# Projection to v and dt as seven block products instead of eight, moved behind the first B, C and x tiles, in a hybrid SSD and attention layer

## The chip, the cores and the metric

The kernel runs on one core of one Trainium2 chip. The metric is the device time of one execution in microseconds (us), the median of several runs. The engines named below are TensorE (PE in the profile; its weight loads are PEld), VectorE (DVE), ScalarE (ACT), GpSimd (POOL) and SyncE (SP, which issues most DMAs). An engine works through its own instructions in order; engines wait for each other through semaphores.

## The reference

One layer of a bidirectional encoder over 512 tokens and a model width of 1024, in float32. All projections of the input come from one matrix product; its columns are split into the parts that the two branches use:

```python
u = h @ w_in                      # x: 512 x 1024
z, xbc, dt_f_raw, dt_b_raw, q, k, v, gate_logits = split(u, ...)
y_ssd = ssd_branch(z, xbc, dt_f_raw, dt_b_raw, ...) @ w_proj_ssd
y_att = attention_branch(q, k, v) @ w_proj_attn
```

In the SSD branch `xbc` (the columns x, B and C) passes a centred convolution over five tokens and SiLU; `dt` is a softplus of its raw columns, 32 heads for each of two directions. From dt come the decays: cumulative sums of `dt * a` over chunks of 128 tokens. The attention branch needs q, k and v (12 heads of 64, so v has 768 columns). Gate, output projection, two LayerNorms and a feed-forward layer of width 4096 follow.

What the change touches is the product of x (512 x 1024) with the 832 columns of v (768) and dt (64).

## The kernel before

**Precision.** A float32 operand is split into a high part `h` (a copy rounded to the matmul's float32r) and a low part `l` = operand minus `h`. A product is three matmuls: h·h, l·h and h·l. The high part is a cast on ACT, the low part a subtraction on DVE (in `Stream.prep`, L107 and L108, for weights; in `split_x`, L227 and L228, for x).

**Weights.** The class `Stream` brings weight tiles in the order of their use: `load` issues the DMA into one of three buffers `wraw`, `prep` splits it into one of two buffers each of `wh` and `wl`, `get` hands out one tile, splits the next and loads up to three ahead. The split is traced under a raised priority: `PRIO = 100` places ahead of where it stands in the program.

**The v/dt stage** (`v_dt_stage`) comes first. Its weights are eight tiles of 128x832, one for each 128 rows (k) of x. For each k and each of four token chunks, x is the stationary operand and the weights move, in three matmuls of 512 columns (`ps_va`, v) and three of 320 (`ps_vb`, the rest of v and dt). All eight PSUM banks accumulate over k. At the end ACT copies the banks to `vs`, four DMAs write v to `dr_v` in DRAM, where the attention picks it up much later, and a chain on ACT and DVE makes dt and `tok` from the dt columns (L266 to L280), with two loads of activation tables (L275, L276).

**B, C and x0 to x3** follow (`plan0`). Each is a column tile: the weights are stationary, x moves, 24 matmuls of 512 columns (`quarters`, L138). `evict` reads the PSUM bank: the convolution is one ACT pass, four DVE steps (L317), a Tanh on ACT (L318) and one more DVE step (L319). Three PSUM banks with the tag `mm` take these tiles in turn. Behind x1 the first matmuls of `cumsum_stage` (L286 to L294) read `tok`; the transposes (L299) follow within x2.

**Order.** Instructions of an engine are ordered by a planner that takes by priority, which is the order of tracing unless raised, what its own timing has ready. From the SSD groups on, TensorE's order is the written one (`manual_schedule`); for the stages above it is the planner's, with `issue_after` as a tie for the cumulative sums. Behind that come four SSD groups with further column tiles between their steps, the attention with projections, and the feed-forward layer. The last one (from 680 us) already multiplies in blocks: seven products per block pair, with sums of blocks by DVE and by adding DMAs on POOL (L1208), and operands split on ACT and DVE (L1233 to L1240).

Of the kernel before, what the change touches and what calls it, by code (L numbers as in the profile page):

```python
# [16 lines left out]
P = 128  # L17
# [17 lines left out]
TAIL = 4  # L35
QT = 1.36
# [9 lines left out]
def hybrid_layer_kernel(ctx: ExitStack, tc: tile.TileContext, t: dict, out: bass.AP):  # L46
# [27 lines left out]
    class Stream:  # L74
# [6 lines left out]
        def load(self, i):  # L81
            if i < len(self.srcs) and i not in self.raw and (self.end is None or i < self.end):
                ap, width, hold = self.srcs[i]
                r = wp.tile([P, 1024], F32, name=f"wraw{i}", tag="wraw", bufs=3)
                if i:
                    dma.dma_start(r[:, :width], ap)
                else:
                    act.dma_start(r[:, :512], ap[:, :512])
                    dma.dma_start(r[:, 512:width], ap[:, 512:])
                self.raw[i] = r  # L90

        def prep(self, i):
            if i < len(self.srcs) and i not in self.hl and (self.end is None or i < self.end):
# [11 lines left out]
                with tc.high_priority(PRIO):  # L105
                    if i:
                        act.copy(h[:, :width], r[:, :width])  # L107
                        dve.tensor_sub(l[:, :width], r[:, :width], f32(h[:, :width]))  # L108
                    else:
                        dve.tensor_copy(h[:, :512], r[:, :512])  # L110
                        self.second = act.copy(h[:, 512:width], r[:, 512:width])
                        dve.tensor_sub(l[:, :512], r[:, :512], f32(h[:, :512]))
                        dve.tensor_sub(l[:, 512:width], r[:, 512:width], f32(h[:, 512:width]))
                self.hl[i] = (h, l)

# [39 lines left out]
    yp_ctx = ExitStack()  # L155
    yp = yp_ctx.enter_context(tc.tile_pool(name="yp", bufs=1, side="right"))
    ys = [yp.tile([P, S], F32, name=f"y{j}", tag="y", bufs=17) for j in range(16)]
# [15 lines left out]
    sp = pa.enter_context(tc.tile_pool(name="sp", bufs=2))  # L173
# [21 lines left out]
    for k in range(KT):  # L195
        ws.add(t["w_vd"][k], 832)
# [11 lines left out]
    xr = []  # L208
    for k in range(KT):
        xr.append(sp.tile([P, S], F32, name=f"xr{k}", tag="x", bufs=8))  # L210
        if k:
            dma.dma_start(xr[k], t["xT"][:, k, :])
        else:
            dma.dma_start(xr[k][:, :256], t["xT"][:, k, :256])
            dma.dma_start(xr[k][:, 256:], t["xT"][:, k, 256:])
        if k < 3:
            ws.load(k)
    dma.dma_start(vec, t["vec"])
    dma.dma_start(dtv, t["dtv"].to_broadcast([P, P]))
    dma.dma_start(tri, t["tri"][:, 1:6, :])  # L220
    dma.dma_start(ident, t["tri"][:, 0, :])

    def split_x(k):
        if k < KT:
            with tc.high_priority(PRIO):
                for cs in ((slice(0, S),) if k else (slice(0, 256), slice(256, S))):
                    act.copy(xh[k][:, cs], xr[k][:, cs])  # L227
                dve.tensor_sub(xl[k], xr[k], f32(xh[k]))  # L228
# [10 lines left out]
    def v_dt_stage():  # L239

        pv = [ps_tile("mm", f"ps_va{i}", 3) for i in range(3)] + [ps_tile("tp", "ps_va3", 3)]
        pd = [ps_tile("tp", f"ps_vb{i}", 3) for i in range(2)] + [ps_tile("y", f"ps_vb{i}", 2) for i in (2, 3)]
        split_x(0)
        ws.prep(0)
        with tc.issue_after(ws.second.ins):
            split_x(1)
        for k in range(KT):
            wh, wl = ws.get()
            split_x(k + 2)
            for i in range(NCH):  # L250
                xk = [(xh[k][:, i * P:(i + 1) * P], xl[k][:, i * P:(i + 1) * P])]
                if k:
                    mm3(pv[i], xk, [(wh[:, :512], wl[:, :512])], False, k == KT - 1)
                    mm3(pd[i][:, :320], xk, [(wh[:, 512:832], wl[:, 512:832])], False, k == KT - 1)
            if k == 0:
                for n, (l, r) in enumerate(((xh, wh), (xl, wh), (xh, wl))):
                    for ps_, cs in ((pv, slice(0, 512)), (pd, slice(512, 832))):
                        for i in range(NCH):
                            pe.matmul(ps_[i][:, :cs.stop - cs.start], l[0][:, i * P:(i + 1) * P], r[:, cs], start=(n == 0), stop=False)
        na = sp.tile([P, 64], F32, name="na", tag="acc", bufs=2)  # L260
        act.activation(na, dtv[:, 64:128], AF.Exp)
        dve.tensor_scalar(na, na, -1.0, None, op0=ALU.mult)
        tl = lambda n: sp.tile([P, NCH, 64], F32, name="dt" + n, tag=n, bufs={"G1": 4, "U": 2, "sq": 2}.get(n, 1))
# [1219 lines left out]
```

## Time and profile before

| | |
|---|---|
| median of three runs | 989.39 us (988.30 to 989.45) |
| the profiled execution | 988.57 us, span 986.8 us |
| TensorE busy | 976.1 us, 99% |
| VectorE busy | 787.0 us, 80% |
| ScalarE busy | 597.2 us, 61% |
| GpSimd busy | 71.7 us, 7% |
| granted TensorE clock | 0.997 |

The span runs from the first to the last instruction; the time around it (1.8 us) belongs to the execution but to no instruction. Busy time of TensorE counts overlapping matmuls once, so 99% means hardly any gap, and not that each matmul is at its peak. The page also has 40 slices with tenths of busy time, groups of instructions, the chain of work that ended last and the DMA queues. A row of a timeline gives start and duration in us, then engine, line, operation, output<-inputs, shape and count, and in brackets the idle time before it and who ended it. A row of one tile's instructions gives shortest, median and longest duration in ns, and the first and the last start in us.

### The profile page before, as it was taken

The numbers are of one execution on the slowest core, as the hardware profiler recorded it, in microseconds if no ns is written. First come the engines' busy times: TensorE is split into PE (matmuls) and PEld (weight loads), VectorE is DVE, ScalarE is ACT, GpSimd is POOL, SyncE is SP. The second block draws the span as 40 slices with busy tenths as digits, with TensorE's granted clock in tenths as the row PEclk, the third lists the DMA queues.
The fourth block names the chain that finished last, engine by engine and source line by source line (L and its number), as shares of the span: only waits on it lengthen the run. The fifth ranks groups of instructions, "written<-read, shape, count | busy, mean of one in ns | idle before, by whom it ended". The sixth has DMA issues, their size and how long they took to land.

```text
span 986.8 us, 14803 instructions
## 1 busy us (share of the span) xinstructions
PE 976.1 (99%) x5471; PEld 835.6 (85%) x5471; DVE 787.0 (80%) x1224; ACT 597.2 (61%) x1140; POOL 71.7 (7%) x74
## 2 busy tenths in 40 slices
PE   9999999999999999999999999999999999999997
PEld 7888888888888888788778888889989998989986
DVE  4296998698998899997788258498898898898757
ACT  4454696369856995695765344147666566666620
POOL 0000100030012101202000000000200110110000
PEclk9999999999999999999999999999999999999998
DMA  7436367325752484374773249313953854671322
GB/s 246 155 116 174 111 201 215 108 86 171 213 154 86 151 241 139 129 245 139 257 221 108 83 156 308 130 44 111 251 151 129 211 131 168 175 170 44 110 83 86
DMA packets 56808, 153.09 MB, mean 155 GB/s; under 512 B 7456, under 2 KB 8736, under 8 KB 56480
## 3 DMA queue, kind: packets, MB, share of 16 engines
q1 hardware_dynamic: 53136, 139.30, 43.6%
q0 software_dynamic: 3456, 12.58, 6.9%
q8 instruction: 43, 0.70, 0.3%
q10 hardware_dynamic: 144, 0.26, 0.1%
q14 instruction: 29, 0.24, 0.1%
HBM read 128.25 MB, written 11.30 MB: 141 GB/s over the span
## 4 chain that ended last, share of the span: by engine, by line
PE 91%; DVE 4%; issue 2%; ACT 1%; DMA 1%; POOL 0%; SPq 0%; DVEq 0%; POOLq 0%; ACTq 0%
PE ps_pa L138 9%; PE ps_x L138 8%; PE ps_z L138 8%; PE ps_x L1124 8%; PE ps_g L138 8%; PE ps_z L1124 4%; PE ps_k L138 3%; PE ps_q L138 3%; PE ps_pX L148 2%; PE ps_pX L149 2%; PE ps_pX L150 2%; PE ps_y L1124 2%; PE ps_B L138 2%; PE ps_yo L550 2%; PE ps_u L138 2%
## 5 line engine op out<-in xcount | busy, mean ns | idle before, releaser
L108 DVE TENSOR_TENSOR wl<-wraw,wh 128x1024 fp32r<-128x1024 f32 (+1 forms) x113 | 140.5, 1249 | 75.6 <-ACT wh L107 58.6
L107 ACT CAST wh<-wraw 128x1024 fp32r<-128x1024 f32 (+1 forms) x113 | 116.5, 1036 | 92.7 <-PE ps_vb L150 16.6
L1240 DVE TENSOR_TENSOR cl<-wq_B,ch 128x1024 fp32r<-128x1024 f32 x42 | 51.2, 1220 | 14.1 <-ACT ch L1239 13.6
L1239 ACT CAST ch<-wq_B 128x1024 fp32r<-128x1024 f32 x42 | 44.1, 1050 | 23.4 <-PE ps_pX L150 16.8
L138 PE MATMUL ps_pa<-yh,wh 128*128 128x512 f32 x128 | 51.7, 404 | 0.0
L138 PE MATMUL ps_g<-xh,wh 128*128 128x512 f32 x128 | 50.6, 395 | 0.0
L138 PE MATMUL ps_x<-xh,wh 128*128 128x512 f32 x128 | 50.5, 394 | 0.0
L138 PE MATMUL ps_z<-xh,wh 128*128 128x512 f32 x128 | 50.4, 393 | 0.0
L138 PE MATMUL ps_g<-xl,wh 128*128 128x512 f32 x128 | 49.9, 390 | 0.0
L138 PE MATMUL ps_x<-xl,wh 128*128 128x512 f32 x128 | 49.9, 390 | 0.0
L138 PE MATMUL ps_z<-xl,wh 128*128 128x512 f32 x128 | 49.9, 389 | 0.0
L1208 POOL DMA_DIRECT2D wq_B<-wq_B x24 | 20.8, 866 | 393.1 <-DMA wq_B<-in_w_dn_dram 227.0
L138 PE MATMUL ps_pa<-yl,wh 128*128 128x512 f32 x128 | 48.4, 393 | 0.0
L317 DVE SCALAR_TENSOR_TENSOR acc<-ps_x,vec,acc 128x510 f32<-128x510 f32 (+1 forms) x64 | 47.6, 743 | 0.8 <-ACT acc L315 0.3
L519 ACT ACTIVATE U<-bc,acr 128x128 f32<-128x128 f32 x128 | 42.3, 391 | 8.7 <-DMA bc<-dr_acr 8.6
L521 DVE SCALAR_TENSOR_TENSOR U<-bc,acr,U 128x128 f32<-128x128 f32 x128 | 43.1, 376 | 0.0
L525 ACT ACTIVATE G<-cb,tok 128x128 f32<-128x128 f32 x128 | 41.7, 390 | 0.0
L148 PE MATMUL ps_pX<-ch,ah 128*128 128x512 f32 x96 | 37.6, 392 | 0.0
L149 PE MATMUL ps_pX<-cl,ah 128*128 128x512 f32 x96 | 37.6, 392 | 0.0
L150 PE MATMUL ps_pX<-ch,al 128*128 128x512 f32 x96 | 37.3, 389 | 0.0
L1233 ACT CAST ah<-r 128x1024 fp32r<-128x1024 f32 x21 | 22.1, 1054 | 21.4 <-PE ps_pX L149 14.3
L138 PE MATMUL ps_pa<-yh,wl 128*128 128x512 f32 x128 | 34.8, 392 | 0.0
(857 smaller groups left out, 2787.5 us busy)
## 6 DMA issues: line engine op xcount, KB each, us to landing
wraw<-in_w_in_dram SPq DMA_DIRECT2D x68, 512.0 KB, 3.7
bc<-dr_acr SPq DMA_DIRECT2D x64, 256.0 KB, 4.2
pr<-in_w_up_dram SPq DMA_DIRECT2D x28, 512.0 KB, 5.5
wq_B<-in_w_dn_dram SPq DMA_DIRECT2D x24, 512.0 KB, 4.4
wq_B<-wq_B POOLq DMA_DIRECT2D x24, 512.0 KB, 4.7
be<-dr_ear SPq DMA_DIRECT2D x32, 256.0 KB, 5.2
wraw<-in_w_ps_dram SPq DMA_DIRECT2D x16, 512.0 KB, 3.9
dr_gate<-g SPq DMA_DIRECT2D x16, 256.0 KB, 2.2
```

The source lines that it names most:

```text
L107: act.copy(h[:, :width], r[:, :width])
L108: dve.tensor_sub(l[:, :width], r[:, :width], f32(h[:, :width]))
L138: ins = pe.matmul(ps, l, r, start=(first and n == 0), stop=(last and n == len(seq) - 1))
L148: pe.matmul(ps, lh, rh, start=(first and i == 0), stop=False, skip_group_check=not check)
L149: pe.matmul(ps, lh, rl, start=False, stop=False, skip_group_check=not check)
L150: ins = pe.matmul(ps, ll, rh, start=False, stop=(last and i == n - 1), skip_group_check=not check)
L317: dve.scalar_tensor_tensor(acc[:, o0:o1], ps[:, i0:i1], w(k), acc[:, o0:o1], op0=ALU.mult, op1=ALU.add)
L519: act.activation(U[:, ch(c)], bb[:, ch(c)], AF.Identity, bias=acr[:, c, 32 + h:33 + h])
L521: dve.scalar_tensor_tensor(U[:, ch(c)], bf[:, ch(c)], acr[:, c, h:h + 1], U[:, ch(c)], op0=ALU.subtract, op1=ALU.min)
L1124: pe.matmul(ps[:, LO], w_[:, wk], src[:, x, k0 + k, cs], start=(first and i == 0), stop=(i == 11), skip_group_check=not first)
L1239: act.copy(h, w[:, j, :])
L1240: dve.tensor_sub(l, w[:, j, :], f32(h))
```

## The change

The product of x and the 832 columns is cut in halves: tokens (2 x 256), features (2 x 512) and columns (2 x 416, `VC`). Instead of eight block products there are seven, with sums and differences of blocks as operands (the scheme of Strassen in Winograd's form). Three of them (1, 2 and 4) use a plain block of x, whose split exists; the other four split a sum.

- **B and C come first.** `first_tiles` computes both at once, in six matmuls per k, so that the slices of x are used as they come. The first halves (k = 0 to 3) of their two weight tiles are loaded ahead of x1, the second halves behind x3 (`load_rest`, `prep_rest`). x0 follows; then the seven products, then x1 to x3.
- **Raw x stays** in one tile `xr`, and four quarters of it (`a11` to `a22`) are overwritten with sums by DVE (`v_prepare`). The four weight blocks `wvq` are loaded whole, 128 x 1664 each; DVE adds b12 and then b22 to b11, POOL's adding DMAs add b22 to b12 and later b21 to b11.
- **A product** is two chunks of 128 tokens, each twelve matmuls of 416 columns. Two chains of PSUM banks, X and Z, go on accumulating over several products; after each product ACT copies the running sum out (`vo`, with sign) and a DMA stores it to its block of `dr_v` or adds it there (products 3, 7 and 2, on POOL). The last 64 columns of the right half are dt: DVE adds them up in `xb`.
- **Preparation** of the product after next is traced behind each product, in buffers of two each for the weight parts (`vh`, `vl`) and the x parts (`vs`), with raised priority. The evictions of B, C and x0, with their convolutions, are traced before the first product.
- **TensorE's order** is the written one through all of this. Behind x1 come the cumulative sums, as before.
- **Buffers.** The stage's pool `vq` is closed after the seven products; the buffers of y and most of those of the SSD groups (`sp.late`) are placed where it was, with waits tile by tile. Those of x, B, C, acc and sq are in a pool of their own (`se`) from the start.

```diff
-    for k in range(KT):
-        ws.add(t["w_vd"][k], 832)
...
+        if k == 0:
+            ws.load(0)
+            ws.load(1)
+        elif k == 3:
+            ws.load_rest(0)
+            ws.load_rest(1)
     dma.dma_start(vec, t["vec"])
     dma.dma_start(dtv, t["dtv"].to_broadcast([P, P]))
...
+    for i, c in ((0, 0), (0, 1), (1, 1), (1, 0)):
+        wvq[i, c] = vq.tile([P, 4, VC], F32, name=f"wv{i}{c}")
+        dma.dma_start(wvq[i, c].rearrange("p k n -> p (k n)"), t["w_vd"][i, c])
+        if i == c == 0:
+            ws.load(2)
+            dma.dma_start(tri, t["tri"][:, 1:6, :])
+            dma.dma_start(ident, t["tri"][:, 0, :])
...
+    def first_tiles():
+        split_x(0)
+        ws.prep(0)
+        split_x(1)
+        ws.prep(1)
+        for k in range(2, KT):
+            split_x(k)
+            if k == 3:
+                ws.prep_rest(0)
+                ws.prep_rest(1)
+        two = [(kind, ps_tile("mm", f"ps_{kind}0", 3), ws.get(0)) for kind in "BC"]
         for k in range(KT):
+            wk = slice(k * P, (k + 1) * P)
+            for n, (wx, xx) in enumerate(((0, xh), (0, xl), (1, xh))):
+                for kind, ps, w in two:
+                    pe.matmul(ps, w[wx][:, wk], xx[k], start=(k == 0 and n == 0), stop=(k == KT - 1 and n == 2))
+        return two
...
+        straight = {1: (0, 0), 2: (4, 0), 4: (4, 2)}
+        w_of = {1: b11, 5: b11, 6: b11, 3: b22, 7: b12, 2: b21, 4: b11}
+        a_of = {5: a21, 6: a21, 3: a21, 7: a11}
+        outs = {1: ("X", 0, 0, 1.0), 5: ("Z", 1, 1, 1.0), 6: ("X", 0, 1, -1.0), 3: ("Z", 0, 1, 1.0), 7: ("X", 1, 1, -1.0), 2: ("Z", 0, 0, 1.0), 4: ("X", 1, 0, 1.0)}
+        order = [1, 5, 6, 3, 7, 2, 4]
...
+        def v_prepare(p):
+            with tc.high_priority(PRIO):
+                h = vq.tile([P, 4, VC], F32R, name=f"vh{p}", tag="vh", bufs=2)
+                l = vq.tile([P, 4, VC], F32R, name=f"vl{p}", tag="vl", bufs=2)
+                sa = None
+                if p in a_of:
+                    sa = vq.tile([P, 2, 4, 256], F32R, name=f"vs{p}", tag="vs", bufs=2)
+                    act.copy(sa[:, 0], a_of[p])
+                    dve.tensor_sub(sa[:, 1], a_of[p], f32(sa[:, 0]))
+                act.copy(h, w_of[p])
+                dve.tensor_sub(l, w_of[p], f32(h))
+                if p == 1:
+                    dve.tensor_sub(a21, a21, a22)
+                    dve.tensor_add(b11, b11, b12)
+                elif p == 5:
+                    dve.tensor_sub(a21, a21, a11)
+                    dve.tensor_add(b11, b11, b22)
+                    pool.dma_start(b12, b22, accum_op=ALU.add)
+                elif p == 6:
+                    dve.scalar_tensor_tensor(a11, a21, -1.0, a22, op0=ALU.mult, op1=ALU.subtract)
+                    dve.tensor_add(a21, a12, a21)
+                    pool.dma_start(b11, b21, accum_op=ALU.add)
...
+                    for n, (x_, w_) in enumerate(((ah, h), (al, h), (ah, l))):
+                        pe.matmul(ps, x_, w_[:, k, :], start=(first and k == n == 0), stop=(k == 3 and n == 2), skip_group_check=not first)
+                i = row * 2 + q
+                st = vq.tile([P, VC], F32, name=f"vo{p}{q}", tag="vo", bufs=4)
+                act.activation(st, ps, AF.Copy, scale=sign)
+                dst = dr_v[i * P:(i + 1) * P, col * VC:min(768, (col + 1) * VC)]
+                src = st[:, :dst.shape[1]]
+                if p in (3, 7, 2):
+                    pool.dma_start(dst, src, accum_op=ALU.add)
+                else:
+                    dma.dma_start(dst, src)
+                if col:
+                    if p in (5, 6):
+                        dve.tensor_add(xb[:, i, :], st[:, VC - 64:], dtv[:, 0:64])
+                    else:
+                        dve.tensor_add(xb[:, i, :], st[:, VC - 64:], xb[:, i, :])
+
+        v_prepare(1)
+        x0 = tile_task("x", 0)
+        next(x0)
+        v_prepare(5)
+        for kind, ps, w in two:
+            evict(kind, 0, ps)
+        for _ in x0:
+            pass
+        for n, p in enumerate(order):
+            v_product(p)
+            if n + 2 < 7:
+                v_prepare(order[n + 2])
...
+    with tc.manual_schedule(engines={mybir.EngineType.PE}):
+        v_dt_stage(first_tiles())
+        vq_ctx.close()
...
+        sp.late = pa.enter_context(tc.tile_pool(name="sp", bufs=2, reuse_waits="tile"))
+        cums = cumsum_stage()
+        for n, _ in enumerate(bg(plan0[3:])):
+            if n in (3, 6):
                 next(cums, None)
```

More of the change, by code (lines that the diff above doesn't have):

```diff
@@ L35 @@
 TAIL = 4
+VC = 416
 QT = 1.36
@@ L105, in prep @@
                 with tc.high_priority(PRIO):
-                    if i:
+                    if i > 1:
                         act.copy(h[:, :width], r[:, :width])
@@ L154, in hybrid_layer_kernel @@
     edge.tile([P, 56], F32, name="edge")
-    yp_ctx = ExitStack()
-    yp = yp_ctx.enter_context(tc.tile_pool(name="yp", bufs=1, side="right"))
-    ys = [yp.tile([P, S], F32, name=f"y{j}", tag="y", bufs=17) for j in range(16)]
+    vq_ctx = ExitStack()
+    vq = vq_ctx.enter_context(tc.tile_pool(name="vq", bufs=1, side="right"))
     ps_ctx = ExitStack()
@@ L172, in hybrid_layer_kernel, with tile @@
     xp = pa.enter_context(tc.tile_pool(name="xp", bufs=1))
-    sp = pa.enter_context(tc.tile_pool(name="sp", bufs=2))
+    se = pa.enter_context(tc.tile_pool(name="se", bufs=2))
+    class Work:
+        late = None
+        def tile(self, shape, dt, name, tag, bufs):
+            home = se if tag in ("sq", "x", "acc", "B", "C") else self.late
+            return home.tile(shape, dt, name=name, tag=tag, bufs=bufs)
+    sp = Work()
     plan0 = [("B", 0), ("C", 0)] + [("x", j) for j in range(4)]
@@ L261, in v_dt_stage @@
         act.activation(na, dtv[:, 64:128], AF.Exp)
         dve.tensor_scalar(na, na, -1.0, None, op0=ALU.mult)
-        tl = lambda n: sp.tile([P, NCH, 64], F32, name="dt" + n, tag=n, bufs={"G1": 4, "U": 2, "sq": 2}.get(n, 1))
-        xb, e, w1, d1 = tl("G1"), tl("G2"), tl("U"), tl("sq")
-        for i in range(NCH):
-            dve.tensor_add(xb[:, i, :], pd[i][:, 256:320], dtv[:, 0:64])
-            vs = sp.tile([P, 2, S], F32, name=f"vs{i}", tag="be", bufs=2).rearrange("p a s -> p (a s)")
-            act.copy(vs[:, 512:768], pd[i][:, 0:256])
-            act.copy(vs[:, 0:512], pv[i])
-            dma.dma_start(dr_v[i * P:(i + 1) * P, :], vs[:, :768])
+        e, w1, d1 = [vq.tile([P, NCH, 64], F32, name="dt" + n) for n in ("e", "w1", "d1")]
@@ L583, in run @@
                     lb = False
-    v_dt_stage()
-    for n, _ in enumerate(bg(plan0)):
-        if n == 4 * CS + 3:
-            cums = cumsum_stage()
-        if n in (4 * CS + 3, 4 * CS + 6):
-            with tc.issue_after(last_mm[0].ins):
+    with tc.manual_schedule(engines={mybir.EngineType.PE}):
+        v_dt_stage(first_tiles())
+        vq_ctx.close()
+        yp_ctx = ExitStack()
+        yp = yp_ctx.enter_context(tc.tile_pool(name="yp", bufs=1, side="right", reuse_waits="tile"))
+        ys = [yp.tile([P, S], F32, name=f"y{j}", tag="y", bufs=17) for j in range(16)]
+        sp.late = pa.enter_context(tc.tile_pool(name="sp", bufs=2, reuse_waits="tile"))
+        cums = cumsum_stage()
+        for n, _ in enumerate(bg(plan0[3:])):
+            if n in (3, 6):
                 next(cums, None)
```

84 lines of the change are left out of this document (47 added, 37 removed).

## The prediction

> **What bounds the kernel now.** I read the head of the page first, then the windows of the first 70 us, because the change lies there. All times are microseconds.
>
> ```profile
> span 986.8 us, 14803 instructions
> PE 976.1 (99%) x5471; PEld 835.6 (85%) x5471; DVE 787.0 (80%) x1224; ACT 597.2 (61%) x1140; POOL 71.7 (7%) x74
> ```
>
> ```profile
> core 0: us, PE busy (x) PEld busy (x) DVE busy (x) ACT busy (x) POOL busy (x), PEclk, DMA share, GB/s
> 0.00:10.00 10.00, 8.80 (x34) 5.60 (x34) 4.02 (x7) 4.58 (x7) 0.34 (x6) 1.00 0.76 252
> 10.00:20.00 10.00, 9.85 (x53) 8.70 (x53) 6.01 (x11) 5.50 (x9) 0.00 (x0) 1.00 0.81 289
> 20.00:30.00 10.00, 10.00 (x55) 8.80 (x54) 2.88 (x3) 1.90 (x3) 0.00 (x0) 1.00 0.36 120
> 30.00:40.00 10.00, 10.00 (x55) 8.82 (x54) 2.71 (x5) 2.68 (x4) 0.00 (x0) 1.00 0.33 105
> 40.00:50.00 10.00, 10.00 (x48) 8.38 (x47) 2.85 (x7) 7.63 (x14) 0.00 (x0) 1.00 0.61 224
> 50.00:60.00 10.00, 10.00 (x46) 8.29 (x45) 9.72 (x14) 4.94 (x8) 0.00 (x0) 1.00 0.43 145
> 60.00:70.00 10.00, 10.00 (x52) 8.40 (x51) 9.82 (x15) 5.54 (x9) 0.00 (x0) 1.00 0.33 107
> ```
>
> The reader should see three things. TensorE is the bound everywhere, so a saved matmul is saved time unless TensorE then waits. The only stretch with idle VectorE (DVE) is the v/dt stage, at 2.7 to 2.9 of 10. From 50 on, where the convolutions of B, C and x run, DVE is at 9.7 to 9.8 of 10. And DMA is busiest (0.76, 0.81) in the first 20 us, when x and the first weights come in.
>
> The matmul spacing comes from first and last starts, and from the chain of waits, which merges matmuls that follow each other.
>
> ```profile
> 4.71 1.46 PE L259 MATMUL ps_va<-wh,xh 128*128 128x512 f32 x4
> ...
> 9.60 0.40 PE L148 MATMUL ps_va<-wh,xh 128*128 128x512 f32 x1
> ...
> 57.92 0.39 PE L138 MATMUL ps_x<-xh,wh 128*128 128x512 f32 x1
> ...
> 63.36 0.38 PE L286 MATMUL ps_cum<-tok,tri 128*128 128x128 f32 x2
> ```
>
> ```profile
> L148 PE MATMUL ps_va<-wh,xh x28: 393/393/398, 9.6 to 40.4; 128*128 128x512 f32 x28
> ```
>
> ```profile
> 47.20 5.44 PE ps_C L138 x24
> 52.64 10.88 PE ps_x L138 x48
> ```
>
> L148 recurs 28 times from 9.6 to 40.4, once per chunk of three 512-column and three 320-column matmuls: 30.8 / 27 = 1.14; one wait of about 0.3 at 10 us is in it, without it 1.13. The 32 chunks therefore cost 36.1. A column tile (24 matmuls of 512) costs 5.44. B starts at 41.6, the tile x1 at 57.92, and the cumulative sums, which need dt, at 63.36. These last two times are what the change must move.
>
> **The change, part by part.**
>
> **TensorE.** 192 matmuls become 168 of 416 columns. No row shows 416, but it lies exactly halfway between 512 and 320, so by interpolation 24 of them cost as much as four chunks, 4.51, and seven products 31.6. Removed: 4.5. Bounds: 24 x 0.227 = 5.44 a product if 416 paid as 512 (then 38.1, a loss of 2.0), and 24 x 0.15 = 3.6 if it paid as 320 (a gain of 11). I take the middle because both forms scale with columns.
>
> **The start.** Now v needs a new slice of x every 4.5; the B and C tiles in front need one every six matmuls, 1.36. So x must arrive faster.
>
> ```profile
> 7.14 0.62 ACT L227 CAST xh<-xr 128x512 fp32r<-128x512 f32 x1 [1.73 <-DMA xr<-in_xT_dram]
> ...
> 8.15 0.89 ACT L107 CAST wh<-wraw 128x832 fp32r<-128x832 f32 x1 [0.39 <-DMA wraw<-in_w_vd_dram]
> ```
>
> ```profile
> L227 ACT CAST xh<-xr x9: 405/616/622, 4.0 to 13.2; 128x512 fp32r<-128x512 f32 x7, 128x256 fp32r<-128x256 f32 x2
> L228 DVE TENSOR_TENSOR xl<-xr,xh x8: 681/684/693, 5.2 to 14.5; 128x512 fp32r<-128x512 f32 x8
> ```
>
> Slice x1 was cast at 7.14 with 0.95 MB queued up to and with it, the next weight at 8.15 with 1.38 MB, the last slice at 13.2 with 3.38 MB. So from 7.14 on 0.4 MB land per us. In the new order 1.05 MB stand up to x1 (7.4), 3.15 to the last slice (12.6), 4.16 to the first v weight block (15.2), 4.68 to x0's weights (16.5), 5.93 and 6.78 to the blocks (0,1) and (1,1) (19.6 and 21.7). B's first matmul needs the whole slice 0, so about 5.0. At k = 1 it waits for the cast of x1 (8.0); from there seven steps of 1.36 and 0.2 for x1's low half give an end of B and C at 17.8, against 15.9 without waits: 1.9 lost. Before, step k = 0 took 4.89 (9.60 - 4.71) instead of 4.51, and the wait at 10 us was 0.3; 0.7 of that old loss goes. x0's weight cast (16.5 + 1.05) is just in time, and x0 ends at 23.25. If x1's cast goes ahead of C's weight cast on ScalarE (ACT), C's first matmul waits until 8.6 and B and C end at 19.2. If the transfers do not limit, they end at 15.9.
>
> [...]
>
> **Side engines.** Each product needs a high and a low part of a weight block (128x1664), four sums of x quarters and two of weight blocks are made on DVE (two more by adding DMAs), and four products split an x operand of 1024.
>
> ```profile
> L107 ACT CAST wh<-wraw x12: 887/890/1050, 8.2 to 56.7; 128x832 fp32r<-128x832 f32 x7, 128x1024 fp32r<-128x1024 f32 x5
> L108 DVE TENSOR_TENSOR wl<-wraw,wh x11: 1024/1026/1226, 9.1 to 55.3; 128x832 fp32r<-128x832 f32 x7, 128x1024 fp32r<-128x1024 f32 x4
> ```
>
> ```profile
> 52.28 3.10 DVE L317 SCALAR_TENSOR_TENSOR acc<-ps_B,vec,acc 128x510 f32<-128x510 f32 x4
> ...
> 56.42 0.69 DVE L319 SCALAR_TENSOR_TENSOR B<-B,acc 128x512 f32<-128x512 f32 x1
> ```
>
> DVE: 0.684 at 512 and 1.226 at 1024 give 1.06 ns a column, so 1.90 at 1664. ACT: 0.616 and 1.05, so 1.59. DVE work in the stage: nine times 1.90 (seven low parts, two block sums) and eight times 1.22 (four low parts of x, four x sums) is 26.9, one of the 1.22 before 16.8 (the first block's landing and its high part, 15.2 + 1.59). Beside it stand three convolutions at 3.7 (11.1), low weights of x0, x1 and x2 (3.7) and eight additions to the dt columns at 0.22 (1.8): 43.5. TensorE, unhindered, gives from 14.5 (x split: ten low parts of 0.69 that DVE makes one after the other behind x1's cast) to 60.3 (cumulative sums: 23.25 + 31.6 + 5.44) 45.8. So DVE, idle before, is nearly full; it is the new second bound. Followed product by product with the preparations ahead of the convolutions, DVE is never free between 16.8 and 37: the third product's low weights are there at 32.7, wanted at 32.6; the fourth's low x at 37.0, wanted at 37.0. One convolution step that slips in costs 0.75. I take 0.8, one step, for such waits; bounds 0 and 7.9 (the slower rival below: 62.8 - 54.85).
>
> The kernel holds a stage of the same make, seven products with split operands and adding DMAs, further on. Its six 40-us windows from 680 to 920 sum to:
>
> ```profile
> sum 240.00, PE 240.00 PEld 220.57 DVE 209.14 ACT 156.13 POOL 20.80; mean PE 40.00 PEld 36.76 DVE 34.86 ACT 26.02 POOL 3.47
> ```
>
> DVE at 87% there leaves TensorE without idle time. That speaks for a small wait, but 43.5 of 45.8 is 95%.
>
> **Adding DMAs.**
>
> ```profile
> wq_B<-wq_B POOLq DMA_DIRECT2D x24, 512.0 KB, 4.7
> ...
> dr_v<-vs SPq DMA_DIRECT2D x4, 384.0 KB, 4.0
> ```
>
> ```profile
> L714 SPq DMA_DIRECT2D vc<-dr_v x1: 560/560/560, 487.9 to 487.9; - x1
> ```
>
> An add of 512 KB lands after 4.7, so one of 832 KB within some 7.6; b12 is wanted three products (13) later, b11 likewise: hidden. The eight stores and six adds into the v scratch have until 488. POOL has no work in any window from 10 to 70. On SP a store waits for its eviction, and a weight load queued behind it comes up to a product (4.5) late; the next weights are wanted two tiles (10.9) on. All this costs nothing; with the cover gone a late add costs at most its 7.6. The waits for the stage's released buffers fall on tiles first written behind the cumulative sums, more than a tile after the last reader: nothing.
>
> **dt.** The last dt addend comes from the fifth product, two products (9.0) and one tile (5.4) before the cumulative sums.
>
> ```profile
> 41.77 0.23 DVE L266 TENSOR_TENSOR dtG<-ps_vb,dtv 128x64 f32<-128x64 f32 x1 [0.90 <-PE ps_vb L150]
> ...
> 45.95 1.28 ACT L275 ACT_TABLE_LOAD   x1
> ...
> 50.80 0.43 DVE L280 TENSOR_TENSOR tok<-tok,na 128x256 f32<-128x256 f32 x1
> ```
>
> That chain took 9.5 (41.77 to 51.23) and was done 12 before its use. Now 14.4 are there. In the forecast it is ready: 0.
>
> **Sum.** x1 starts at 23.25 + 31.6 + 0.8 = 55.65 instead of 57.92: 2.3 less. Profiled time 988.57 - 2.3 = 986.3. That execution lies 0.8 below the median of 989.39, and the median less 2.3 is 987.1; I take 986.6.
>
> **Rivals.**
>
> **Whole eighth** (15%). Transfers do not limit and DVE never waits: 41.6 - 4.5 is kept, and up to 0.7 of the old start loss: 988.57 - 4.5 = 984.1, with the same 0.3 towards the median 984.4. For it: from 7.14 on the rows land 0.4 MB per us. Against it: the 1.36 pace of B and C in front. [...]
>
> **dt late** (24%). The convolutions of B, C and x0 stand before the dt chain in the program. If DVE does them first it is full to 16.8 + 42.3 = 59.1, and the chain from its first table load on (45.95 to 51.23: 5.3) ends at 64.4; TensorE, in written order, stands at the cumulative sums from 60.3 to 64.4, 1.0 later than before. 989.5, no change. For it: DVE at 95%.
>
> **Convolutions first** (17%, slower). They stand ahead of the preparations on DVE. Then product after product waits, and TensorE runs at DVE's pace: 16.8 + 25.7 + 11.1 + 3.7 + 1.0 (additions by then) = 58.3 for the last low part, 4.5 for the last product, x1 at 62.8 instead of 57.9: 993.5. It decides as soon as one convolution of 3.7 goes in front of the third preparation, where DVE has no slack; from then on the gain of 3.1 without waits is gone. For it: the convolutions are traced earlier than five of the seven preparations. Against it: these are raised by 100 places.
>
> **Clock** (4%; another 4% for a buffer or an adding DMA that comes late, 3 or more). The granted clock is 1.00 in every row above. If a wait at the start took it down to half for B and C, their 10.9 would double at worst: 997.5. [...]
>
> The chances left to the forecast are 36%. Differences of 0.2% (2.0 us) are what a measurement of this kernel can tell. Faster: three quarters of the forecast, all of the first rival and a little of the rest, 0.45. Same: most of the second rival, a quarter of the forecast, 0.32. Slower: the last two and a part of the second, 0.23. The range 984.0 to 992.0 leaves out the far end of the slower cases and a little of the fastest; the forecast's own range is 985.3 to 987.6.
>
> **What would show it.** B's first matmul near 5.0 and the last of C near 17.8; a product's matmuls at 0.188 and a product at 4.5; x1 at 55 to 56; DVE above 9 of 10 from 17 to 60; the cumulative sums right behind x1. Wrong if TensorE waits for a low part (DVE, the line of the block split) for more than 2 in all, or for tok, or if it waits at the start beyond k = 1.

## The result, and the profile after

The changed kernel takes 995.75 us (median of six runs, 993.94 to 998.90) against 989.32 (988.30 to 989.45): ratio 1.0070, 95% interval 1.0052 to 1.0088. It is slower by 6.4 us; 986.6 was forecast, and the time lies beyond the range. The profiled execution took 994.32, 5.75 more than the one of before. All times below are microseconds.

The head of the page of the changed kernel, and its windows of the first 70 us (columns as in the prediction):

```profile
span 992.5 us, 14819 instructions
...
PE 975.2 (98%) x5447; PEld 835.8 (84%) x5447; DVE 804.8 (81%) x1238; ACT 607.7 (61%) x1150; POOL 78.7 (8%) x82
```

```profile
0.00:10.00 10.00, 5.20 (x12) 1.84 (x12) 3.58 (x7) 4.38 (x8) 0.34 (x6) 1.00 0.74 237
10.00:20.00 10.00, 10.00 (x39) 8.12 (x39) 9.34 (x14) 7.29 (x10) 0.00 (x0) 1.00 1.02 401
20.00:30.00 10.00, 9.49 (x44) 7.82 (x43) 9.58 (x8) 4.19 (x5) 1.00 (x1) 1.00 0.86 315
...
50.00:60.00 10.00, 8.06 (x43) 7.64 (x43) 7.79 (x16) 5.15 (x10) 4.12 (x5) 1.00 0.47 49
60.00:70.00 10.00, 10.00 (x53) 8.94 (x52) 3.50 (x7) 6.95 (x11) 1.12 (x2) 1.00 0.67 163
```

TensorE was busy for 8.80 of the first 10 us before and is now for 5.20; VectorE, at 6.0 and 2.9 of 10 from 10 to 30 before, stands at 9.3 and 9.6 there. Nearly all that is lost is lost by 63 us, as the timeline of TensorE in the changed kernel shows, cut to the rows after an idle time and to the marks of the prediction.

```profile
8.83 0.80 PE L280 MATMUL ps_B<-xh,wh 128*128 128x512 f32 x1 [3.61 <-ACT xh L252]
9.42 0.63 PE L280 MATMUL ps_C<-xh,wh 128*128 128x512 f32 x1
...
12.57 0.58 PE L280 MATMUL ps_B<-xl,wh 128*128 128x512 f32 x1
12.99 0.40 PE L280 MATMUL ps_C<-xl,wh 128*128 128x512 f32 x1
...
21.66 0.39 PE L280 MATMUL ps_C<-xh,wl 128*128 128x512 f32 x1
22.55 0.50 PE L148 MATMUL ps_x<-xh,wh 128*128 128x512 f32 x1 [0.51 <-ACT wh L110]
...
28.12 0.35 PE L338 MATMUL ps_vX<-vh,xh 128*128 128x416 f32 x1
...
47.45 0.46 PE L338 MATMUL ps_vX<-vh,vs 128*128 128x416 f32 x1 [0.53 <-DVE vs L305]
...
54.00 0.46 PE L338 MATMUL ps_vZ<-vh,xh 128*128 128x416 f32 x1 [1.94 <-ACT vo L341]
...
63.18 0.39 PE L148 MATMUL ps_x<-xh,wh 128*128 128x512 f32 x1
...
68.66 0.38 PE L385 MATMUL ps_cum<-tok,tri 128*128 128x128 f32 x2
```

```profile
28.28 4.52 PE ps_vX L338 x24
```

The second fence is the chain of waits: a product of 24 matmuls of 416 takes 4.52, as forecast. Against the forecast, B starts 3.8 late (8.83 instead of 5.0) and x0 starts 4.75 late (22.55 instead of 17.8); x1 is 7.5 late (63.18 instead of 55.65), and from there little is added: x1 is 5.3 later than before (57.92) and the span 5.7 longer.

ScalarE's timeline shows what B waited for.

```profile
4.13 0.41 ACT L252 CAST xh<-xr 128x256 fp32r<-128x256 f32 x1 [1.67 <-DMA xr<-in_xT_dram]
5.50 0.62 ACT L114 CAST wh<-wraw 128x512 fp32r<-128x512 f32 x1 [0.96 <-DMA wraw<-in_w_in_dram]
7.85 2.01 ACT L252 CAST xh<-xr 128x512 fp32r<-128x512 f32 x4 [1.73 <-DMA xr<-in_xT_dram]
...
21.45 1.05 ACT L110 CAST wh<-wraw 128x1024 fp32r<-128x1024 f32 x1 [1.25 <-PE ps_B L280]
```

Behind the first half of slice 0 come C's weights and then slice 1, whose transfer lands at 7.85; the second half of slice 0, landed by then, is cast behind them, inside the row of four casts. In the old kernel `issue_after(ws.second.ins)` held slice 1 back, and the change dropped that line. The last row is a wait that I had not seen: the third tile's `wh` is one of two buffers, and the last of B's matmuls that uses it has to release it.

### The profile page after: what moved, and what is told of

It reads as the page before. It is cut to its first block, busy times and chain, and to the rows that moved or that the text cites. A ratio compares the mean times of both kernels' runs of the same rounds, so it can differ in the third digit from the quotient of the medians.

```text
span 992.5 us, 14819 instructions
## 1 busy us (share of the span) xinstructions
PE 975.2 (98%) x5447; PEld 835.8 (84%) x5447; DVE 804.8 (81%) x1238; ACT 607.7 (61%) x1150; POOL 78.7 (8%) x82
## 4 chain that ended last, share of the span: by engine, by line
PE 83%; DVE 7%; issue 4%; ACT 4%; DMA 2%; POOL 1%; SPq 0%; DVEq 0%; ACTq 0%; POOLq 0%
PE ps_pa L148 9%; PE ps_x L1227 8%; PE ps_g L148 7%; PE ps_z L148 7%; PE ps_x L148 6%; PE ps_z L1227 4%; PE ps_q L148 3%; PE ps_pX L158 2%; PE ps_pX L159 2%; PE ps_pX L160 2%; PE ps_y L1227 2%; PE ps_u L148 2%; PE ps_k L148 2%; PE ps_pZ L158 2%; PE ps_pZ L159 2%
## 5 line engine op out<-in xcount | busy, mean ns | idle before, releaser
L111 DVE TENSOR_TENSOR wl<-wraw,wh 128x1024 fp32r<-128x1024 f32 x104 | 131.1, 1265 | 59.8 <-ACT wh L110 41.6
L110 ACT CAST wh<-wraw 128x1024 fp32r<-128x1024 f32 x104 | 108.2, 1045 | 75.7 <-PE ps_z L148 10.7
```

## The experiments

**The start, the evictions, the warm-up.** Four kernels, each from the changed one. Ratios go by the kernel before as it was timed beside each of them; its median there was 988.6 to 989.0, against 989.32 above. The first holds slice 1 behind slice 0:

```diff
-        split_x(0)
+        cast = split_x(0)          # split_x returns its last cast
         ws.prep(0)
-        split_x(1)
+        with tc.issue_after(cast.ins):
+            split_x(1)
```

> Only the order of two casts on ScalarE is changed: the second half of slice 0 of x ahead of slice 1. Theory (the loss is a late start): B's first matmul starts near 5.1 instead of 8.83, the half-rate spacing of 0.43 at its start goes, B and C end near 18.2 instead of 21.9, and the tile x1 starts near 59.5 instead of 63.18; the time falls by 3.7 to about 992. Rival (VectorE is the bound of the whole stage): the products wait for their low parts instead, x1 stays within 1 of 63.2 and the time within 1 of 995.75.

Measured 994.02, ratio 1.0060 (1.0044 to 1.0075): 1.7 less, half of what was expected. B started at 6.68 instead of 8.83, still at the slow spacing (0.43 up to 10.43). x1 started at 59.47, where 59.5 was expected, but in part by luck: its first eviction of product 3 also went ahead of the cast that held it up, so that the wait ahead of product 2 was gone. The cumulative sums then waited 1.76, for dt. The second lets the cast for the product after next queue behind an eviction that TensorE needs sooner:

```diff
             if n + 2 < 7:
-                v_prepare(order[n + 2])
+                with tc.issue_after(out_of[order[n - 1]].ins) if n else ExitStack():
+                    v_prepare(order[n + 2])    # out_of[p]: p's last eviction
```

> Only the order on ScalarE is changed: the eviction of a product stands ahead of the casts for the product after next but one. Theory: the wait of 2.3 ahead of the sixth product (product 2) was the order on ScalarE alone; it goes, and the time falls by 2.1 to about 993.6. Rival: the same wait turns up at the next product for its low weights or at the cumulative sums for tok, since VectorE is full; no change within 0.5.

Measured 992.75, ratio 1.0041 (1.0027 to 1.0055): 3.0 less, where 2.1 was expected; the wait ahead of product 2 fell from 1.94 to 0.44. The third changes only `WARM = 9` to `WARM = 25` multiplications of zeros ahead of B.

> 25 instead of 9 matmuls on zeros ahead of the work, so that TensorE is never idle between 5.2 and 8.8; nothing else. Theory: B's first nine matmuls at a spacing of 0.43 ran at half clock after 3.6 of idle time; now they run at 0.227 from the first on and the time falls by 2.0 to about 993.8. Rival: they were slow because their operands came late; spacing and time stay.

Measured 991.33 (990.29 to 992.16), ratio 1.0024 (1.0014 to 1.0035): 4.4 less, over twice what was expected, and the runs lie closer together. B and C were spaced 0.23 from the second matmul on, but for one wait of 0.29. That is only a part of the gain: x0 starts 1.8 earlier in the profile (20.78 instead of 22.55) and x1 3.7 (59.49). The rest goes with the wait of 1.94 ahead of product 2, which is gone here too, although no line about evictions was changed: the planner put product 3's evictions ahead of the cast that held them up. The fourth holds the first two edits together.

> Both orders of ScalarE changed (slice 0 and evictions). Theory: the two gains add up, 3.7 + 2.1, x1 starts near 57.4 and the time is about 990, even with the kernel before. Rival (VectorE full): the second gain is lost behind the first, x1 near 59.5 and about 992.

Measured 991.13 (990.81 to 992.08), ratio 1.0028 (1.0017 to 1.0039). So the start and one eviction account for 4.6, and the kernel before, at 988.71 beside it, is still 2.4 ahead.

**What is left of the start.** From the fourth kernel: C's weight cast behind slice 0 too, and TensorE kept busy with zeros until slice 1 is there.

```diff
         with tc.issue_after(cast.ins):
-            split_x(1)
-        ws.prep(1)
+            ws.prep(1)
+            split_x(1)
...
+        # k = 0: B's three matmuls, 2 of zeros, C's three, 7 of zeros; then k = 1 to 7 as before
```

> The run with both the slice-0 order and the eviction order, and besides: C's weight cast goes behind slice 0's second cast too, and TensorE is kept busy with multiplications of zeros, two behind B's first three matmuls and seven behind C's first three, until slice 1 is there. Theory (TensorE runs at half rate for some 4 us after any idle gap of 1.5 us, and the first slice's cast need not wait for C's weights): B starts at about 5.2 instead of 6.40, the matmuls of B and C are spaced 0.23 from slice 1 on, C ends near 18.3 instead of 19.6, the time is 1.2 to 2.0 below that run, near 989.5. Rival (the half rate has nothing to do with the gap, or the slices of x set the pace of B and C): C ends near 19.6 as before and the time stays at 991.

Measured 992.93 (990.69 to 994.53): no gain. B started at 5.00 and C's last matmul was at 18.57, as expected, but then x0 waited for its weights and TensorE fell to half rate. The timeline of TensorE in this kernel:

```profile
18.57 0.39 PE L287 MATMUL ps_C<-xh,wl 128*128 128x512 f32 x1
21.13 0.50 PE L148 MATMUL ps_x<-xh,wh 128*128 128x512 f32 x1 [2.18 <-ACT wh L110]
...
22.39 0.56 PE L148 MATMUL ps_x<-xl,wh 128*128 128x512 f32 x1
22.74 0.63 PE L148 MATMUL ps_x<-xh,wh 128*128 128x512 f32 x1
...
25.73 0.46 PE L148 MATMUL ps_x<-xl,wh 128*128 128x512 f32 x1
26.03 0.40 PE L148 MATMUL ps_x<-xh,wh 128*128 128x512 f32 x1
```

The spacing is 0.43 instead of 0.23 between 22.74 and 25.73, with no wait inside. The next kernel puts x0's weights into a buffer of the products' x parts (`vs`) instead of B's and loads them one place earlier.

```diff
+                    w2 = vq.tile([P, 2, 4, 256], F32R, name="wx0", tag="vs", bufs=2)
+                    h, l = (w2[:, a].rearrange("p k n -> p (k n)") for a in range(2))
```

> e5_start, and x0's weights are cast into two buffers of their own instead of B's, and loaded one place earlier. Theory (the third tile waits for B's last matmul to release its cast weights): the wait before x0's first matmul, 0.5 to 0.9, is gone and the time falls by as much, to about 988.8. Rival (x0's weights come too late from memory anyway): the wait stays, now behind the load.

Measured 992.51 (990.88 to 993.21), within the spread of e5_start, where 988.8 was expected. The wait before x0 is gone, but in its profile B's and C's first matmuls ran at half rate, 0.43 apart until 9.45, so x0 still started at 20.77. (An expectation below puts 11.2 there; that was a misreading.)

**Is it the eighth or the arrangement?** The same arrangement with eight plain block products (`order = [(0, 1), (1, 1), (0, 0), (1, 0)]`, the four weight blocks, with four token chunks each; four weight casts, no sums, no adding DMAs):

> The arrangement of e6_own (B, C and x0 first, the projection behind them in blocks) with eight plain block products instead of seven: no sums, no adding transfers, four casts of weights instead of seven, none of x. Theory (the seven products do save an eighth of TensorE's time, and it is the arrangement around them that costs more than that): eight products take 36.1 without a wait against 31.7 plus 1.2 of waits, so this run is 3.3 to 4.5 longer than e6_own, near 992.5. Rival (the sums and casts cost what the product saves): it is as fast as e6_own within 1.

Measured 990.93 (990.68 to 991.17), ratio 1.0021 (1.0011 to 1.0031). Eight were not slower than seven, and their executions spread by 0.5, where those of e6_own spread by 2.3. From its timeline, the first matmul of the eight and the first of x1:

```profile
24.15 0.35 PE L320 MATMUL ps_v<-vh,xh 128*128 128x416 f32 x1
...
60.20 0.39 PE L151 MATMUL ps_x<-xh,wh 128*128 128x512 f32 x1
```

That is 36.1 without a wait. A part of the difference to e6_own is the start, which ran at full rate here (0.23 apart from 9.37 on, x0 at 18.71). The eighth was there to be saved, and something around the seven products gave it back. First suspect, x0's convolution on VectorE, traced behind the products instead:

```diff
-        evict("x", 0, ps0)      # right behind x0's matmuls
...
+        evict("x", 0, ps0)      # behind the last step of dt
```

> e6_own, and x0's convolution and silu are written out behind the seven products and the dt chain instead of ahead of them. Theory (the waits inside the products, 0.27 + 0.53 + 0.43 in the run with both orders, are casts that VectorE brings late because convolution steps of 0.6 to 0.9 stand ahead of them): they shrink to under 0.5 together and the time falls by up to 0.8 against e6_own. Rival (those casts wait for their own inputs, the sums before them): the waits stay and the time is the same, or longer by the convolution's 3 us where it now delays x1 to x3.

Measured 991.49 (990.24 to 993.38), within the spread of e6_own; in its profile the products began 1.9 earlier (24.33 instead of 26.20) and the product waits were 1.8 and 1.1 instead of 1.3. So from a start like that of the eight (24.33), seven products with their waits brought x1 to 60.00, against 60.20. Then a start with 14 matmuls of zeros and no idle time on TensorE up to the products, and three kernels on top of it.

> e6_own with 14 instead of 9 multiplications of zeros ahead of B and five behind C's first three, none behind B's. Theory (TensorE reaches the full rate only after about 4 us of work without a gap; the nine end right at that point, so that a gap of 0.23 at 6.05 started the count anew in e6_own, whose first 22 matmuls ran at half rate until 11.2): B starts near 6.2, everything from B on is spaced 0.23, C ends near 18.4 instead of 20.8, and the executions lie closer together than e6_own's 2.3 us. Of these 2.4 a part comes back as waits for VectorE, which is busy without a pause from 16 to 55 in e6_own: the time falls by 0.5 to 2 against e6_own, to some 991. Rival (VectorE does not bind): all 2.4 arrive, 990.

Measured 992.19 (990.52 to 994.19), within the spread of e6_own, where 0.5 to 2 less was expected. C ended near 18.8, about as expected. That the full rate comes after some 4 us of work, counted anew after a gap, was my estimate from e6_own's trace, and no run shows it: fourteen zeros without a gap took 4.52 in e10_notaps and 5.96 in e17_sums, and in e5_start the same nine zeros of 4.02 as in e6_own, with a gap of 0.33 behind them, were followed by matmuls 0.23 apart (from 6.35 on). In TensorE's timeline the time came back as waits:

```profile
35.40 0.46 PE L350 MATMUL ps_vX<-vl,vs 128*128 128x416 f32 x1 [1.54 <-DVE vl L319]
...
45.66 0.46 PE L350 MATMUL ps_vX<-vh,vs 128*128 128x416 f32 x1 [1.08 <-DVE vs L317]
...
65.25 0.46 PE L398 MATMUL ps_cum<-tok,tri 128*128 128x128 f32 x2 [0.36 <-PE ps_x L151]
```

The next leaves the convolution's shifted steps out for three tiles.

```diff
-        for k, (o0, o1, i0, i1) in ((0, ...), (1, ...), (3, ...), (4, ...)):
+        for k, (o0, o1, i0, i1) in () if ci in (0, 16, 20) else ((0, ...), ...):
```

> e9_steady without the four shifted multiply-adds of the convolution for B, C and x0: 12 VectorE instructions of 0.66 each, 7.9 us, are left out, and with them a part of the computation. Theory (with the start mended, VectorE's queue of casts, sums and convolution sets the pace of the seven products): the waits inside the products go from about 3 to under 0.7 and the last tile before the cumulative sums ends 2 to 3 earlier; the cumulative sums then wait for dt. Rival (each late cast waits for its own inputs): the waits stay.

Measured 990.33 (988.22 to 991.53), 1.9 less. The second wait went, the first stayed at 1.58: the theory was half right. Three sums of x on GpSimd:

```diff
-                    dve.tensor_sub(a21, a21, a22)
+                    pool.tensor_sub(a21, a21, a22)      # and the sums with a11 and a12
```

> e9_steady with the three plain sums of halves of x on GpSimd instead of VectorE, 3.7 us less for VectorE. Theory (VectorE binds): the product waits shrink by 1 to 2 and the time by as much, if GpSimd's sums take under 3 us each; the second one stands ahead of product 5's weights in no queue of VectorE any more. Rival: GpSimd is so slow, or slows VectorE so much, that products 6 and 3 wait for the sums, and the time is longer by 2 or more.

Measured 996.46 (993.94 to 997.32), slower, as the rival had it. GpSimd took 2.66, 2.40 and 5.09 for sums that VectorE does in 1.22, two splits of 1.88 on VectorE took 4.02 and 3.41 beside them, and a product then waited 2.81. The cumulative sums one tile later:

> e9_steady with the cumulative sums one tile later, behind the third instead of the second x tile. Theory (dt's chain ends near 62.5 and becomes the next bound when the products end earlier): a wait of 0 to 1.5 before the cumulative sums in e9_steady is gone and the time falls by that. Rival (the sums are needed early by the first group): the time stays, or the first group waits for them by up to 5.

Measured 991.82 (990.84 to 994.05): unclear beside e9_steady, because its profiled execution fell to half rate after a wait of 1.75 (below). But it started the cumulative sums without a wait, and the first group did not wait for them.

**Order of the side work.** The wait that the left-out steps did not touch ends a chain: low part of a block, sum into the block, high part, low part, sum, high part, low part. The end of it in e9_steady, from the timelines of VectorE and ScalarE:

```profile
29.39 1.89 DVE L325 TENSOR_TENSOR wv<-wv,wv 128x1664 f32<-128x1664 f32 x1
...
31.59 3.28 ACT L318 CAST vh<-wv 128x1664 fp32r<-128x1664 f32 x2
...
33.46 3.69 DVE L319 TENSOR_TENSOR vl<-wv,vh 128x1664 fp32r<-128x1664 f32 x2
```

The sum is followed by the high parts and then by the low part that product 6 waits for until 35.40. What else stood in front was the convolutions and x1's weights, needed at 59 and split at 31. The next kernel holds the convolutions of B, C and x0 until product 3 is evicted and x1's weights until product 7 is.

```diff
+            if p == 7:
+                with tc.issue_after(out_of[7].ins):
+                    ws.prep(3)
+                with tc.issue_after(out_of[3].ins):
+                    for kind, ps, w in two + [("x", ps0, None)]:
+                        evict(kind, 0, ps)
```

> e9_steady with the convolutions of B, C and x0 held back until the fourth product is evicted and the cast of x1's weights until the fifth is; nothing is left out. Theory (the casts for the next product are late because such work stands ahead of them on VectorE and ScalarE): the waits inside the products, 1.54 and 1.08 in e9_steady, fall below 0.5 together and the products end near 56 instead of 59.2; dt, which has its own chain behind them, then decides and the cumulative sums start at 62 to 64 instead of 65.3; time 988.5 to 990. Rival (a product's casts need as long as a product on ScalarE and VectorE with two buffers, 4.5 in a row, whatever stands around them): the waits stay above 1.5.

Measured 994.86 (994.30 to 995.60), slower, although its one product wait is 1.28: the convolutions now stood ahead of dt's chain, and the cumulative sums waited 3.2. So dt's chain was raised to directly behind product 7:

```diff
+            if p == 7:
+                with tc.high_priority(PRIO):
+                    ...     # the chain of dt, moved here from behind the loop
```

> e14_behind with the chain of dt written out, at high priority, right behind the fifth product, the last that dt needs, instead of behind all seven. Theory: dt is there by 60 instead of 62 to 64, the cumulative sums start right behind x1, near 61.5 to 62.5, time 987 to 988.5, below the kernel before. Rival (ScalarE still serves the evictions first): no more than 0.5 below e14_behind.

Measured 991.76 (991.58 to 992.95), 3.1 less but not the 987 to 988.5 expected. Two of TensorE's waits, from its list of waits (line, what ended the wait, us in all, times, longest):

```profile
PE ps_cum L406 <- issue: 2.0, 1, 2.0
PE ps_vX L350 <- DVE vl L319: 1.3, 1, 1.3
```

The first is for dt, although the list names no releaser: in VectorE's timeline `tok` is done at 64.82, and the cumulative sums start at 64.92. Holding the last evictions behind dt's chain as well:

```diff
+                with tc.issue_after(out_of[0].ins) if p in (2, 4) else ExitStack():   # dt's last Exp
                     out_of[p] = act.activation(st, ps, AF.Copy, scale=sign)
```

> e15_chain with ScalarE's evictions of the last two products held until the chain of dt has passed ScalarE. Theory (dt waits behind evictions that TensorE has not finished, 2.3 and 0.8 in e9_steady): another 0 to 1.5 less than e15_chain, cumulative sums right behind x1. Rival: the products' banks or the results in memory are then late and it is the same or up to 2 longer.

Measured 992.42 (990.63 to 997.17): no gain. The last two waits were then taken away together, from e15_chain:

```diff
-                    dve.tensor_sub(a21, a21, a11)
-                    dve.tensor_add(b11, b11, b22)
+                    with tc.issue_after(out_of["s"].ins):      # the sum b11 + b12
+                        dve.tensor_sub(a21, a21, a11)
+                    out_of["t"] = dve.tensor_add(b11, b11, b22)
...
-                    dve.scalar_tensor_tensor(a11, a21, -1.0, a22, ...)
+                    with tc.issue_after(out_of["t"].ins):
+                        dve.scalar_tensor_tensor(a11, a21, -1.0, a22, ...)
...
-            if n in (3, 6):
+            if n in (7, 10):
                 next(cums, None)
```

> e15_chain with the two sums of halves of x that are not needed next put behind the sums of weights (2.4 us earlier for the chain: sum, cast, residual, sum, cast, residual that ends in the sixth product's weights), and with the cumulative sums one tile later, behind the third x tile. Theory (the last waits are that chain and dt): no wait over 0.3 between B's second slice and the first group, x1 starts at 56.0 instead of 57.3, the first group's transposes at 74.5 to 75.5 (76.1 in the kernel before), the time is 987 to 988.3, below the kernel before by 0.7 to 2. Rival: another wait takes their place, or the later cumulative sums make the first group wait, and it stays at 990 or above.

Measured 988.64 (987.93 to 989.72), ratio 1.0002 (0.9992 to 1.0011): level with the kernel before (988.61 beside it), 7 below the changed one. The 0.7 to 2 below the kernel before that were expected did not come. TensorE has no idle time in any window from 10 to 70; four of the seven windows:

```profile
0.00:10.00 10.00, 8.81 (x28) 4.18 (x29) 4.05 (x8) 4.62 (x8) 0.34 (x6) 1.00 0.74 240
10.00:20.00 10.00, 10.00 (x46) 8.25 (x45) 9.18 (x13) 7.41 (x10) 0.00 (x0) 1.00 1.02 386
20.00:30.00 10.00, 10.00 (x51) 9.17 (x50) 9.44 (x7) 3.98 (x5) 1.00 (x1) 1.00 1.04 360
...
60.00:70.00 10.00, 10.00 (x50) 8.43 (x49) 9.52 (x15) 5.46 (x10) 0.00 (x0) 1.00 0.22 75
```

```profile
24.48 0.35 PE L352 MATMUL ps_vX<-vh,xh 128*128 128x416 f32 x1
...
56.30 0.39 PE L151 MATMUL ps_x<-xh,wh 128*128 128x512 f32 x1
...
74.51 0.60 PE L562 MATMUL ps_bt<-ident,B 128*128 128x128 f32 x4
```

The second fence, its timeline, has the seven products from 24.48 to 56.30: 31.8, against 36.1 for the eight. The first group's transposes start 1.6 earlier than in the kernel before (76.1 there), and so does TensorE's last matmul (977.58 against 979.19); the span is only 0.6 shorter, because in this execution 4.3 instead of 3.3 lie between VectorE's last instruction and the end. That is not scatter of one execution: e18_early's trace, below, has the same 4.3, and in both the slowest store of the result lands 3.1 after its issue. Of the 18 other traces each has 3.2 to 3.3, and no such store takes more than 2.4. What in these two kernels makes it late is open. Eight products in the arrangement of e17_sums were not run. Last, C's first weights behind slice 1:

```diff
-        if k == 0:
-            ws.load(0)
-            ws.load(1)
+        if k < 2:
+            ws.load(k)
...
+        for m, k in ((0, 0), (0, 1), (1, 0), (1, 1)):     # B's slices 0 and 1, then C's
```

> e17_sums with C's first weights loaded and cast behind slice 1 of x instead of ahead of it, and TensorE taking B's first two slices, then C's. Theory (TensorE waits for slice 1, whose place in the transfers decides the start): slice 1 is cast near 7.2 to 7.8 instead of 8.6 to 9.2, x0 and the products come 0.8 to 1.2 earlier and the time falls to 987.5 to 988. Rival (the later C weights take slice 1's place as what is late, or VectorE's first casts for the products become the next wait): the same as e17_sums within 0.3.

Measured 989.09 (988.32 to 990.76), ratio 1.0003, the same as e17_sums, as the rival had it. C's weights came 0.43 late, product 6 waited 0.56 again and x1 stood at 56.6. No run beat the kernel before.

**Why executions of the changed kernel lie so far apart.**

> The changed kernel once more, profiled. If it is a longer execution (above 996): theory (each wait of TensorE of about 1.5 or more may be followed by some 4 us at half rate, by chance) expects a stretch of matmuls at about 0.34 to 0.43 behind the wait for the eviction of product 3, in the profile of 994.3 absent; rival: the same waits, only longer ones, with no such stretch. Below 996 it says nothing.

It took 995.83, just under the 996 of the expectation, but its trace shows the stretch all the same. Its timeline of TensorE, with the same wait as in the execution of 994.32:

```profile
54.19 0.53 PE L338 MATMUL ps_vZ<-vh,xh 128*128 128x416 f32 x1 [1.94 <-ACT vo L341]
54.52 0.55 PE L338 MATMUL ps_vZ<-vh,xl 128*128 128x416 f32 x1
...
57.29 0.55 PE L338 MATMUL ps_vZ<-vh,xh 128*128 128x416 f32 x1
57.64 0.45 PE L338 MATMUL ps_vZ<-vh,xl 128*128 128x416 f32 x1
57.93 0.35 PE L338 MATMUL ps_vZ<-vl,xh 128*128 128x416 f32 x1
```

```profile
46.00:56.00 10.00, 7.55 (x35) 6.72 (x35) 9.78 (x13) 5.04 (x6) 1.57 (x2) 0.92 0.08 21
56.00:66.00 10.00, 10.00 (x49) 9.69 (x48) 3.34 (x11) 7.09 (x13) 3.67 (x5) 0.91 1.01 186
```

Ten matmuls spaced 0.345 instead of 0.188 cost 1.6, and the granted clock shows 0.92 and 0.91 where the other execution has 1.00. The cumulative sums are at 70.3 instead of 68.7, 1.6 later, of which 0.2 lay ahead of the wait already. So the same wait of 1.94 cost some 1.5 more in one execution than in the other. The granted clock of whole executions goes the same way: 0.998 to 0.999 in the three of 993.9 to 994.9, 0.996 here, and 0.992 to 0.993 in the three of 996.6 to 998.9. That these three had more such stretches fits, but none of them was traced.

## Why the prediction was wrong

**TensorE's term was right.** Seven products took 31.8 without waits (forecast 31.6), spaced 0.188 as interpolated, and the removal is worth 36.1 - 31.8 = 4.3 (forecast 4.5).

**The step that failed is the start**, "B's first matmul needs the whole slice 0, so about 5.0", with "1.9 lost". I reckoned when transfers land and left ScalarE's order as the program's text has it; I even named the variant that slice 1's cast goes ahead of another, but of C's weights, and priced it at 1.4. It went ahead of half of slice 0. The ledger up to x0's first matmul: forecast 17.8; 2.0 more because k = 0 is done behind slice 1 instead of ahead of it (0.45 of it because slice 1 landed at 7.85 and not at 7.4); 2.1 because the first nine spacings of B's and C's matmuls took 4.16 instead of 2.04 (8.83 to 12.99); 0.65 for x0's weight buffer, which B has to release (C's last start, 21.66, plus 0.23, to 22.55): 22.55, as measured. These 4.75 are the greater part of the 7.5 by which x1 was late; nearly all the rest lies in the products.

**The rival "Clock"** was this half rate, set at 4%. It came behind a wait of 3.61. The granted clock of the windows, 1.00, didn't show it; the spacing of the matmuls did, 0.43 instead of 0.23. It cost 2.1 and not 10.9, because it ended after nine spacings. That it was the idle time and not late operands, e3_warm shows: with zeros up to B's first matmul the spacing was 0.23.

**Waits inside the products** were mis-sized: 0.8 was taken, all of it VectorE's. From 28.12 to 63.18 are 35.06, 3.2 more than the 31.8 without waits. The largest part, some 2.1 around a wait of 1.94, was not VectorE's but ScalarE's, a term that the sum does not have: product 3's evictions stood behind a cast that waited for product 7 to release its buffer. ScalarE's timeline of the changed kernel has both:

```profile
51.95 1.58 ACT L306 CAST vh<-wv 128x1664 fp32r<-128x1664 f32 x1 [3.24 <-PE ps_vX L338]
53.44 0.92 ACT L341 ACTIVATE vo<-ps_vZ 128x416 f32<-128x416 f32 x2
```

I had looked at VectorE's order alone. Its own waits, in products 6 and 7, came to some 1.2, near the 0.8. In the kernels with a faster start they grew (1.54 and 1.08 in e9_steady). That VectorE is the second bound was right, but a sum of its work (43.5 of 45.8) couldn't say where a wait falls: the serial chain of in-place sums and casts decided. Removing 7.9 of other work left its wait in place (e10_notaps), and putting the sums of the chain first took it away (e17_sums).

**dt in time** was right by luck. VectorE's timeline of the changed kernel has dt's last step end 0.36 ahead of the cumulative sums.

```profile
67.88 0.42 DVE L379 TENSOR_TENSOR tok<-tok,na 128x256 f32<-128x256 f32 x1
```

From the end of product 7 (51.9) to there are 16.4, where the prediction counted 14.4 up to the cumulative sums and 9.5 for the chain; in this execution only the wait of 1.94 ahead of product 2 left room for it. Without that wait dt was late in e1_slice0 (1.76), and later in e14_behind (3.2) and e15_chain (2.0), though not in e3_warm, e4_both and e10_notaps. That is the mechanism of the rival "dt late".

**Adding DMAs** were hidden, as forecast (within 7.6); from the list of DMA issues of the changed kernel's trace:

```profile
wv<-wv POOLq DMA_DIRECT2D x2, 832.0 KB, 6.2
```

With all waits taken away x1 starts at 56.30, where 55.65 was forecast. For x1 the forecast thus describes the kernel of e17_sums, with all its edits of order and buffers, and not the one that was changed. For the time it describes neither: in e17_sums x1 is 1.6 earlier than in the kernel before, and the medians are the same.

## What to carry to other kernels

A stage with little slack is forecast by walking the order of each in-order engine, not by summing its work: what stands ahead of the instruction that the bound engine needs next, and which buffer it waits for. When TensorE's work shrinks and moves forward, ask which of the former covers, a slow consumer of the first transfers here, goes with it. Here the eighth saved on the bound engine was worth nothing until the split, sum and eviction chains around it ran ahead of it, and even then the kernel was level with the one before.

## What was not expected of the hardware

**The rate of TensorE after a gap.** I had set half rate at 4%, for the start alone. It came there, and behind shorter gaps too: TensorE ran at about half its rate for some 3.4 to 3.9 after 1.47 (e1_slice0: 0.43 spacing from 6.68 to 10.43, behind the warm-up), after 1.75 (e12_late, 35.48 to 39.40) and 2.18 (e5_start, 22.39 to 25.73, setting in 1.3 behind the gap), and after 1.94 in one execution (54.19 to 57.64) and not in the other. Two lines of e12_late, from its timeline:

```profile
35.48 0.46 PE L350 MATMUL ps_vX<-vl,vs 128*128 128x416 f32 x1 [1.75 <-DVE vl L319]
...
39.40 0.36 PE L350 MATMUL ps_vX<-vl,vs 128*128 128x416 f32 x1
```

The matmuls between them are 0.345 apart instead of 0.188. After another 1.75 (e7_conv), 1.76 (e1_slice0), 1.54 (e9_steady) and shorter waits amid full-rate work no such stretch was seen, so the "any idle gap of 1.5 us" in e5_start's expectation, my reading of the 1.47, doesn't hold. What decides whether a stretch follows a gap, no run here shows.

**GpSimd** took 2.40 to 5.09 for a sum of 128x1024 that VectorE does in 1.22 (e11_pool).
